# A third pair of k-tiles by Strassen's scheme in the second halves of the down projection

## The chip, the cores and the metric

The kernel runs on one core of a Trainium2 chip. The metric is the time of one execution on the device in microseconds (us); lower is better. A core has a matrix engine (TensorE, PE in the profile, with its weight loads as PEld), a vector engine (VectorE, DVE), a scalar engine (ScalarE, ACT), GpSimd (POOL) and SyncE (SP), which here only issues DMAs. TensorE accumulates into eight banks of PSUM of 128 x 512 fp32 numbers each; everything else lives in SBUF, with 128 partitions.

## The reference

One layer of a decoder block over 256 tokens with a model width of 2048, all in float32. A mixer of three branches (a conformer convolution, a short convolution, cross-attention into 256 memory tokens), gated and summed, goes through an output projection, and then comes an MLP. The change is in the MLP:

```
h = rms_norm(x, g_mlp_pre)                         # 256 x 2048
f = square(relu(h @ w_up)) @ w_down                # w_up 2048 x 8192, w_down 8192 x 2048
x = x + rms_norm(f, g_mlp_post)
```

## The kernel before

**Precision.** Every float32 factor is split into a high part and the remainder, both in a reduced fp32 type (`F32R`). A product of an activation tile and a weight tile is three matmuls: high by high, high by remainder, remainder by high. This text calls such three matmuls of 512 columns *a product*.

**Weights.** The list `units` is written out by `plan` and `plan_rows` ahead of the program, in the order in which TensorE will want the weights. `in_unit(u)` (L197) hands a unit to the matmuls and calls `fetch(u + LOOK)`, with `LOOK = 4`. Fetching a unit is: a 512 KB load issued by SP into one of six `raw` buffers, a cast on ScalarE to `wh` (L146), and a subtraction on VectorE to `wl` (L147). There are five buffers each of `wh` and `wl`.

**The MLP** runs in four blocks (`blk`, L930) of 2048 of the 8192 inner channels. In each, four groups of the up projection (`channels_first`, 64 matmuls of 512 columns and 64 of 256) fill four banks each. Their results are scaled, put through relu and square and split into `ft` (L940 to L948) while the next group runs. Then the down projection multiplies the block's 2048 channels, sixteen k-tiles of 128, into sums over the blocks in `acc2` (256 x 2048). It does so for the first 1024 columns (`n = 0`, the first halves) and then for the second 1024 (`n = 1`, the second halves), each with one call of `block` (L286, called at L963). In block 3 the second halves are done otherwise, by `tokens_first` for columns 1024 to 1535 and 1536 to 2047, which also ends the kernel.

**A call of `block`** covers 256 tokens (two tiles `t`) by 1024 columns (two halves `q` of 512). A k-tile done plainly, a *row*, is four products, one to each of the four accumulators C11, C12, C21, C22. A *pair* of k-tiles would be eight products; by Strassen's scheme (Winograd's form) it is seven. Its weights come in four units:

- `first` and `second` load the two rows of the pair. Only half of `first` is split. GpSimd then issues an accumulating DMA for each (L149, L151), SBUF to SBUF, that adds one half of a raw row to another; the second one writes into the buffer of the first.
- `outer` (L136 to L139) makes two sums of raw halves with two additions on VectorE, which need the first transfer, and splits them.
- `inner` splits what the two transfers left in the buffer of `first`.

The raw buffers of `first` and `second` are held that long. The activation side of these units are four sums of quarter tiles per pair, made by `down_sums` (L921) while the second up group's results are drained. Products that don't go to a C go to four more banks, P1, P6, P7 and Q5, so a block with pairs uses all eight. At the last of those products `gather` (block 0) or `gather_add` (the others) adds them into `acc2` on VectorE, and behind the block `after_down` (L907) adds the C banks.

**The order of a block's units** is made by `plan_rows` (L101): `lead` plain rows, then the four units of each pair, staggered, with the other rows between them, and one row at the end. With two pairs and `lead=4`, as in all down blocks before, a block has 62 products. The gate blocks of the mixer (`gates`, L665) use the same `block` and `fetch_row`; several of them have three pairs, with `lead=2`.

**Order on the engines.** Tile buffers come from pools (`t8`, 13 buffers of 8 KB per partition; `t1k`, six of 256 columns; small rings beside them). The instructions of each engine are ordered at build time by a planner with its own costs and by priorities: fetching goes ahead (`high_priority`), work in `soon()` further ahead.

Of the kernel before, what the change touches and what calls it, by code (L numbers as in the profile page):

```python
# [9 lines left out]
F32R = mybir.dt.float32r  # L10
# [5 lines left out]
P = 128  # L16
D = 2048
T = 256
KD = D // P
# [7 lines left out]
NC5 = 512  # L27
# [15 lines left out]
X_PAIRS = ((0, 8), (1, 9), (2, 10))  # L43
GATES = ((0, 3), (2, 3), (0, 3))
O_PAIRS = ((0, 4), (1, 5), (2, 6))
D_PAIRS = ((0, 4), (1, 5))
TQ = ((0, 0), (1, 0), (0, 1), (1, 1))
LOOK = 4
PRIO = 400
# [4 lines left out]
def tile_hybrid_block(ctx, tc, x, head, xT, mem, memT, vecs, w_in, w_a_out, w_b_out, w_kv, w_x_out, w_o,  # L54
# [19 lines left out]
    def t8(shape, dt=F32):  # L74
        return big.tile(shape, dt, tag="t8", name=name("t8"))

    def t1k(cols=T, bufs=6):
        return sm.tile([P, cols], F32, tag=f"t{cols}", name=name("s"), bufs=bufs)
# [22 lines left out]
    def plan_rows(w, row0, col0, nk, pairs=(), lead=2, hold=0):  # L101

        taken = [k for p in pairs for k in p]
        rows = [("row", k, None) for k in range(nk) if k not in taken]
        parts = [(4 * j + at, what, k, j) for j, (k0, k1) in enumerate(pairs)
                 for what, k, at in (("first", k0, 0), ("second", k1, 1), ("outer", k0, 4.5), ("inner", k0, 6.5))]
        parts = [p[1:] for p in sorted(parts)]
        order, among = rows[:lead], rows[lead:-1]  # L110
        for n, p in enumerate(parts):
            while n >= hold and among and (len(among) - 0.5) * (len(parts) - hold) >= (len(rows) - 1 - lead) * (len(parts) - n):
                order.append(among.pop(0))
            order.append(p)
        got = []
        for what, k, j in order + among + rows[-1:]:
            units.append((w, row0 + k * P, col0, (what, j), None))
            got.append((what, k, j, len(units) - 1))
        return got, pairs
# [166 lines left out]
    def block(rows, act, forms=None, gathered=None):  # L286

        todo = []
        rows, pairs = rows

        def tile_of(k, t):
            return lambda: [act(k)[:, i, t * P:(t + 1) * P] for i in range(2)]

        def form(j, i):
            return lambda: [f[:, j, i, :] for f in forms]

        for what, k, j, u in rows:  # L300
            if what == "row":
                todo += [(u, f"C{t + 1}{2 - q}", tile_of(k, t), q) for t, q in TQ]
            elif what == "first":
                todo.append((u, "P1", tile_of(k, 0), 1))
            elif what == "second":
                todo += [(u, "C11", tile_of(k, 0), 1), (u, "C12", form(j, 3), 0)]
            elif what == "outer":
                todo += [(u, "P6", form(j, 1), 0), (u, "C21", tile_of(pairs[j][1], 1), 1)]
            else:
                todo += [(u, "Q5", form(j, 0), 1), (u, "P7", form(j, 2), 0)]  # L310

        todo[:8] = sorted(todo[:8], key=lambda x: x[1])
        last = {x[1]: i for i, x in enumerate(todo)}
        end = max((i for c, i in last.items() if c[0] != "C"), default=None)
        acc = {}
        for i, (u, c, a, q) in enumerate(todo):
            wh, wl = in_unit(u)[q]
            ah, al = a()
            first = c not in acc
            if first:  # L320
                acc[c] = bank()
            mm(acc[c], ah, wh, first, False)
            mm(acc[c], ah, wl, False, False)
            mm(acc[c], al, wh, False, i == last[c])
            if i == end:
                with soon():
                    gathered(acc)
            if i % 8 == 7:
                between()
        return acc  # L330
# [31 lines left out]
    def split(src, dst_h, dst_l):  # L362
        nc.scalar.copy(dst_h, src)  # L363
        nc.vector.tensor_tensor(dst_l, src, dst_h.bitcast(F32), ALU.subtract)  # L364

    def pair(tiles):
        return lambda k: tiles[k // 4][:, k % 4]


    g_gate, g_y, g_up, g_dn = {}, {}, {}, {}  # L370
# [27 lines left out]
    for blk in range(4):  # L398
        for g in range(4):
            g_up[blk, g] = plan(w_up, 0, blk * D + g * NC5, gain=V_MLP)  # L400
        for n in range(2):
            if blk < 3 or n == 0:
                g_dn[blk, n] = plan_rows(w_down, blk * D, n * 2 * NC5, KD, D_PAIRS, lead=4)
    for n in (2, 3):
        g_dn[3, n] = plan(w_down, 3 * D, n * NC5)

# [57 lines left out]
    def over_partitions(r, dst):  # L464

        b = bank()
        for t in range(2):
            dg = t1k(P, bufs=2)
            nc.vector.tensor_scalar(dg, ident, r[:, t:t + 1], None, ALU.mult)
            mm(b[:, t * P:(t + 1) * P], ones, dg, t == 0, t == 1)  # L470
        nc.vector.tensor_copy(dst, b[:, :T])
# [232 lines left out]
    for i in range(2):  # L704
        cx = t8([P, 4, KB - 1 + T])
        nc.gpsimd.memset(cx[:, :, 0:KB - 1], 0.0)
        for c, b in enumerate(channels_first(g_sc[i], xg)):
            s = t1k()
# [212 lines left out]
    def down_sums(fd, j, qa, qb):  # L921

        s = t512().rearrange("p (i t) -> p i t", i=4)
        nc.vector.tensor_tensor(s[:, 0, :], qa[:, P:], qb[:, P:], ALU.subtract)
        nc.vector.tensor_tensor(s[:, 1, :], s[:, 0, :], qa[:, :P], ALU.subtract)
        nc.vector.tensor_tensor(s[:, 2, :], qa[:, :P], qa[:, P:], ALU.subtract)
        nc.vector.tensor_tensor(s[:, 3, :], qb[:, :P], s[:, 1, :], ALU.add)
        split(s, fd[:, 0, j], fd[:, 1, j])

    for blk in range(4):  # L930
        f, kept = [], []
        fd = t8([P, 2, len(D_PAIRS), 4, P], F32R)
        for g in range(4):
            first = blk == 0 and g == 0
            if first:
                steps += [stats_2, lambda: over_partitions(r2, r2_bc), keep_x2, load_gq]
            banks = channels_first(g_up[blk, g], pair(h2),
                                   late=turns if first else None)
            ft = t8([P, 4, 2, T], F32R)
            for c, b in enumerate(banks):  # L940
                s = t1k()
                halves(b, s)
                nc.vector.scalar_tensor_tensor(s, s, 0.0, r2_bc, ALU.max, ALU.mult)
                paired = c < len(D_PAIRS)
                q = (sm.tile([P, T], F32, tag="kept", name=name("q"), bufs=len(D_PAIRS)) if g == 0 and paired else t1k())
                nc.vector.tensor_tensor(q, s, s, ALU.mult)  # L946
                split(q, ft[:, c, 0, :], ft[:, c, 1, :])
                if g == 0 and paired:  # L948
                    kept.append(q)
                elif g == 1 and paired:  # L950
                    down_sums(fd, c, kept[c], q)
            f.append(ft)
        if blk == 3:
            res = [t8([P, D]) for _ in range(2)]
            for t in range(2):
                x2[t] = t8([P, D])
                nc.sync.dma_start(x2[t], x2_kept[t])
        forms = [fd[:, i] for i in range(2)]
        for n in range(2 if blk < 3 else 1):
            def part(t, q):  # L960
                return acc2[t][:, (2 * n + q) * NC5:(2 * n + q + 1) * NC5]

            acc = block(g_dn[blk, n], pair(f), forms,  # L963
                        lambda acc: gather(acc, part) if blk == 0 else gather_add(acc, part))
            for t, q in TQ:
                after_down(blk, 2 * n + q, t, acc[f"C{t + 1}{2 - q}"])
        for n in (2, 3) if blk == 3 else ():
            if n == 3:
                def none(acc):
                    pass  # L970

                def d_0(acc):
                    after_down(3, 3, 0, acc[0])
                    rf = row_rsqrt(ssf[0])
                    for n in range(3):
                        finish(0, rf, n * NC5, (n + 1) * NC5)
                    late_rf.append(rf)

                def d_1a(acc):
                    after_down(3, 3, 1, acc[1], 0, T)  # L980

                def d_1(acc):
                    after_down(3, 3, 1, acc[2], T, NC5)
                    rf = row_rsqrt(ssf[1])
                    with tc.issue_after(mean[0]):
                        finish(0, late_rf[0], 3 * NC5, D)
                    for c0, c1 in ((0, 256), (256, 768), (768, 1408), (1408, D)):
                        finish(1, rf, c0, c1)

                tokens_first(g_dn[blk, n], pair(f), late=[none, d_0, none, d_1a, d_1], fine=True)  # L990
            else:
                for t, b in enumerate(tokens_first(g_dn[blk, n], pair(f))):
                    after_down(blk, n, t, b)
# [37 lines left out]
```

## Time and profile before

| | |
|---|---|
| time, median of 3 runs | 1575.07 us (1574.99 to 1575.26) |
| the profiled execution's own time | 1574.08 us |
| its span, first to last instruction | 1572.2 us |
[...]
| PE busy | 1551.4 us, 99% |
| DVE busy | 1245.8 us, 79% |
| ACT busy | 831.5 us, 53% |
| DMA, mean | 206 GB/s |

The span is that of one execution under the profiler; the time of the runs is a little longer than the span, as the profiled execution's own time shows. Busy shares are means over stages with different limits, so a stage is read by itself. In the rows below a line such as `L147` is the line of the kernel that issued the instruction, `out<-in` names the tiles by the program's names, and `<-` behind an idle time names what ended it. For a matmul `bank<-wh,t` is a product whose weights stream (`block`, the down projection and the gates) and `bank<-t,wh` one whose activations stream (the up projection).

### The profile page before, as it was taken

The numbers are of one execution on the slowest core, as the hardware profiler recorded it, in microseconds if no ns is written. First come the engines' busy times: TensorE is split into PE (matmuls) and PEld (weight loads), VectorE is DVE, ScalarE is ACT, GpSimd is POOL, SyncE is SP. The second block draws the span as 40 slices with busy tenths as digits, with TensorE's granted clock in tenths as the row PEclk, the third lists the DMA queues.
The fourth block names the chain that finished last, engine by engine and source line by source line (L and its number), as shares of the span: only waits on it lengthen the run. The fifth ranks groups of instructions, "written<-read, shape, count | busy, mean of one in ns | idle before, by whom it ended". The sixth has DMA issues, their size and how long they took to land.

```text
span 1572.2 us, 21520 instructions
## 1 busy us (share of the span) xinstructions
PE 1551.4 (99%) x7866; PEld 1324.9 (84%) x7866; DVE 1245.8 (79%) x1883; ACT 831.5 (53%) x1170; POOL 55.6 (4%) x75
## 2 busy tenths in 40 slices
PE   8999999999999999999999999999999999999997
PEld 7888888888888888888788988888888888888886
DVE  7888787798898988778776787778778687777785
ACT  7654454554443545455555665456545555456552
POOL 0000000000000010000100000000000000000000
PEclk9999999999999999999999999999999999999999
DMA  9765555587666768558776665776577666776682
GB/s 321 221 206 190 190 163 172 159 234 223 189 189 174 229 187 286 181 174 237 226 259 196 221 191 175 228 240 191 167 234 232 202 190 199 208 236 189 207 259 81
DMA packets 132521, 324.54 MB, mean 206 GB/s; under 512 B 10432, under 2 KB 14784, under 8 KB 131392
## 3 DMA queue, kind: packets, MB, share of 16 engines
q1 hardware_dynamic: 124352, 308.50, 61.7%
q0 software_dynamic: 8064, 14.68, 5.4%
q8 instruction: 61, 1.00, 0.3%
q14 instruction: 44, 0.36, 0.1%
HBM read 304.26 MB, written 4.19 MB: 196 GB/s over the span
## 4 chain that ended last, share of the span: by engine, by line
PE 91%; DMA 3%; DVE 3%; issue 2%; ACT 0%; POOL 0%; SPq 0%; POOLq 0%; DVEq 0%; ACTq 0%
PE bank L84 90%; DMA raw<-raw 2%; DVE wl L147 1%; DMA raw<-in_w_o 1%; DMA t<-in_xT 0%; DMA raw<-in_w_down 0%; DVE t L833 0%; DVE t L364 0%; DVE raw L139 0%; DVE t L672 0%; PE bank L841 0%; ACT wh L146 0%; DVE t L918 0%; DVE wl L169 0%; DVE t L687 0%
## 5 line engine op out<-in xcount | busy, mean ns | idle before, releaser
L84 PE MATMUL bank<-wh,t 128*128 128x512 f32 (+1 forms) x2536 | 778.2, 387 | 0.0
L84 PEld LDWEIGHTS bank<-wh,t 128*128 128x128 f32 x2536 | 474.0, 188 | 96.6 <-DVE t L364 0.5
L146 ACT CAST wh<-raw 128x1024 fp32r<-128x1024 f32 (+1 forms) x328 | 330.2, 1017 | 330.7 <-PE bank L84 246.0
L84 PE MATMUL bank<-wl,t 128*128 128x512 f32 (+1 forms) x1268 | 490.4, 387 | 0.5 <-DVE wl L147 0.5
L84 PE MATMUL bank<-t,wh 128*128 128x512 f32 (+1 forms) x1936 | 464.5, 391 | 6.0 <-ACT wh L163 4.6
L147 DVE TENSOR_TENSOR wl<-raw,wh 128x1024 fp32r<-128x1024 f32 (+1 forms) x328 | 379.6, 1176 | 95.8 <-ACT wh L146 93.7
L84 PEld LDWEIGHTS bank<-t,wh 128*128 128x128 f32 x1936 | 354.9, 189 | 73.5 <-ACT wh L163 4.6
L84 PEld LDWEIGHTS bank<-wl,t 128*128 128x128 f32 x1268 | 238.2, 188 | 48.8 <-DVE wl L147 1.2
L84 PEld LDWEIGHTS bank<-t,wl 128*128 128x128 f32 x1936 | 248.7, 191 | 10.6 <-DVE wl L164 1.1
L163 ACT CAST wh<-raw 128x1024 fp32r<-128x1024 f32 (+1 forms) x161 | 168.1, 1046 | 165.7 <-PE bank L84 152.6
L164 DVE TENSOR_TENSOR wl<-raw,wh 128x1024 fp32r<-128x1024 f32 (+1 forms) x161 | 195.5, 1217 | 73.7 <-ACT wh L163 73.2
L84 PE MATMUL bank<-t,wl 128*128 128x256 f32 (+1 forms) x1936 | 252.0, 283 | 0.9 <-DVE wl L164 0.9
L169 DVE SCALAR_TENSOR_TENSOR wl<-raw,vec,wh 128x512 fp32r<-128x512 f32 x256 | 180.4, 747 | 46.2 <-ACT wh L168 45.7
L168 ACT ACTIVATE wh<-raw,vec 128x512 fp32r<-128x512 f32 x256 | 171.5, 717 | 76.1 <-PE bank L84 57.0
L596 DVE SCALAR_TENSOR_TENSOR t<-a_pad,vec,t 128x256 f32<-128x256 f32 x240 | 103.9, 482 | 0.0
L359 ACT COPY s<-bank 128x256 f32<-128x256 f32 x128 | 45.6, 368 | 54.6 <-PE bank L84 53.2
L360 DVE TENSOR_TENSOR s<-bank,s 128x256 f32<-128x256 f32 x128 | 51.7, 420 | 19.3 <-ACT s L359 19.3
L149 POOL DMA_DIRECT2D raw<-raw x28 | 24.4, 872 | 1025.3 <-DVE wl L147 1014.5
L363 ACT CAST t<-s 128x256 fp32r<-128x256 f32 x88 | 34.2, 401 | 37.7 <-DVE s L946 29.4
L138 DVE TENSOR_TENSOR raw<-raw,raw 128x512 f32<-128x512 f32 x28 | 19.3, 689 | 28.3 <-DMA raw<-raw 27.1
L364 DVE TENSOR_TENSOR t<-s,t 128x256 fp32r<-128x256 f32 x88 | 36.3, 421 | 5.0 <-ACT t L363 3.8
L151 POOL DMA_DIRECT2D raw<-raw x28 | 24.2, 863 | 127.1 <-DMA raw<-raw 108.8
(144 smaller groups left out, 530.6 us busy)
## 6 DMA issues: line engine op xcount, KB each, us to landing
raw<-in_w_in SPq DMA_DIRECT2D x191, 512.0 KB, 4.3
raw<-in_w_up SPq DMA_DIRECT2D x128, 512.0 KB, 4.0
raw<-in_w_down SPq DMA_DIRECT2D x128, 512.0 KB, 4.8
raw<-in_w_kv SPq DMA_DIRECT2D x32, 512.0 KB, 3.9
raw<-in_w_o SPq DMA_DIRECT2D x32, 512.0 KB, 5.3
raw<-raw POOLq DMA_DIRECT2D x56, 256.0 KB, 3.7
raw<-in_w_x_out SPq DMA_DIRECT2D x16, 512.0 KB, 4.6
raw<-in_w_b_out SPq DMA_DIRECT2D x16, 512.0 KB, 5.3
```

The costliest lines, as they stand in the source:

```text
L84: nc.tensor.matmul(o, a, b, start=start, stop=stop)
L146: nc.scalar.copy(h[:, part], raw[:, part])
L147: pace[0] = nc.vector.tensor_tensor(l[:, part], raw[:, part], h[:, part].bitcast(F32), ALU.subtract).ins
L163: nc.scalar.copy(h, raw)
L164: pace[0] = nc.vector.tensor_tensor(l, raw, h.bitcast(F32), ALU.subtract).ins
L168: nc.scalar.mul(h[:, j, :], raw[:, j, :], g)
L169: pace[0] = nc.vector.scalar_tensor_tensor(l[:, j, :], raw[:, j, :], g, h[:, j, :].bitcast(F32), ALU.mult, ALU.subtract).ins
L359: nc.scalar.copy(t, b[:, T:])
L360: nc.vector.tensor_tensor(dst, b[:, :T], t, ALU.add)
L363: nc.scalar.copy(dst_h, src)
L364: nc.vector.tensor_tensor(dst_l, src, dst_h.bitcast(F32), ALU.subtract)
L596: nc.vector.scalar_tensor_tensor(conv[:, c, :], src, w, conv[:, c, :], ALU.mult, ALU.add)
```

## The change

The second halves of the down projection in blocks 0 to 2 take a third pair of k-tiles, (2, 6), by Strassen's scheme, and have two plain rows ahead of the pairs in place of four. The first halves keep two pairs and four rows. The sums on the activation side are made for three pairs in every block, and are kept in two tiles (high and remainder) in place of one. The scratch of 128 columns in `over_partitions` is taken from the ring of 256 columns. The ring `kept`, sized by the number of pairs, has three buffers in place of two.

```
-D_PAIRS = ((0, 4), (1, 5))
+D_PAIRS = ((0, 4), (1, 5), (2, 6))
+DOWN = (2, 3)
...
-                g_dn[blk, n] = plan_rows(w_down, blk * D, n * 2 * NC5, KD, D_PAIRS, lead=4)
+                g_dn[blk, n] = plan_rows(w_down, blk * D, n * 2 * NC5, KD, D_PAIRS[:DOWN[n]], lead=4 - 2 * n)
...
-            dg = t1k(P, bufs=2)
+            dg = t1k()[:, :P]
...
-        split(s, fd[:, 0, j], fd[:, 1, j])
+        split(s, fd[0][:, j], fd[1][:, j])
...
-        fd = t8([P, 2, len(D_PAIRS), 4, P], F32R)
+        fd = [t8([P, len(D_PAIRS), 4, P], F32R) for _ in range(2)]
...
-        forms = [fd[:, i] for i in range(2)]
...
-            acc = block(g_dn[blk, n], pair(f), forms,
+            acc = block(g_dn[blk, n], pair(f), fd,
```

The units of a second-half block, with the product at which each starts (r: row, f, s, o, i: first, second, outer, inner unit of a pair):

```
before  r2 0, r3 4, r6 8, r7 12, f0 16, r8 17, s0 21, r9 23, f1 27, r10 28, o0 32, r11 34,
        s1 38, i0 40, r12 42, o1 46, r13 48, i1 52, r14 54, r15 58, end 62
after   r3 0, r7 4, f0 8, r8 9, s0 13, f1 15, r9 16, o0 20, s1 22, r10 24, i0 28, r11 30,
        f2 34, o1 35, r12 37, s2 41, i1 43, r13 45, o2 49, i2 51, r14 53, r15 57, end 61
```

## Rows read from the trace of the kernel before

**Rows 1.** The page, part 1: busy us of each engine, share of the span, instructions.
```profile
PE 1551.4 (99%) x7866; PEld 1324.9 (84%) x7866; DVE 1245.8 (79%) x1883; ACT 831.5 (53%) x1170; POOL 55.6 (4%) x75
```
**Rows 2.** Waits of PE over the whole span: us in total, times, longest.
```profile
PE bank L84 <- ACT wh L163: 4.6, 1, 4.6
...
PE bank L84 <- DVE wl L147: 0.5, 1, 0.5
```
**Rows 3.** Timeline of PE (start, us, what) where block 0 starts its down projection.
```profile
955.68 0.39 PE L84 MATMUL bank<-wh,t 128*128 128x512 f32 x1
```
**Rows 4.** Timeline of PE where block 0 of the MLP gives over to block 1.
```profile
1040.01 1.98 PE L84 MATMUL bank<-t,wh 128*128 128x512 f32 x8
```
**Rows 5.** Busy us by stage of the MLP; last: clock, DMA share, GB/s.
```profile
997.90:1040.00 42.10, 42.10 (x187) 34.86 (x186) 30.11 (x36) 21.65 (x25) 3.44 (x4) 1.00 0.74 223
...
1062.30:1084.60 22.30, 22.30 (x130) 19.70 (x129) 17.04 (x34) 13.02 (x24) 0.00 (x0) 1.00 0.63 189
1084.60:1106.90 22.30, 22.30 (x130) 19.70 (x129) 19.49 (x42) 14.07 (x26) 0.00 (x0) 1.00 0.65 190
1106.90:1129.10 22.20, 22.20 (x130) 19.61 (x129) 16.22 (x29) 11.87 (x20) 0.00 (x0) 1.00 0.61 189
...
1171.30:1213.40 42.10, 42.10 (x188) 34.85 (x187) 32.78 (x40) 21.64 (x25) 3.44 (x4) 1.00 0.73 218
...
1475.90:1518.10 42.20, 41.69 (x184) 34.22 (x183) 32.64 (x45) 22.62 (x28) 3.44 (x4) 1.00 0.82 251
```
**Rows 6.** DVE groups by shape, MLP blocks: busy us, mean ns, idle before.
```profile
L147 DVE TENSOR_TENSOR wl<-raw,wh 128x1024 fp32r<-128x1024 f32 x112 | 135.5, 1222 | 47.8 <-ACT wh L146 46.4
...
L138 DVE TENSOR_TENSOR raw<-raw,raw 128x512 f32<-128x512 f32 x12 | 8.3, 689 | 9.1 <-DMA raw<-raw 9.1
L147 DVE TENSOR_TENSOR wl<-raw,wh 128x512 fp32r<-128x512 f32 x12 | 8.3, 688 | 2.7 <-ACT wh L146 2.6
...
L364 DVE TENSOR_TENSOR t<-u,t 128x512 fp32r<-128x512 f32 x8 | 5.5, 685 | 0.0
...
L924 DVE TENSOR_TENSOR u<-q,s 128x128 f32<-128x128 f32 x8 | 2.3, 286 | 0.0
```
**Rows 7.** ACT groups by shape, MLP blocks.
```profile
L146 ACT CAST wh<-raw 128x1024 fp32r<-128x1024 f32 x112 | 117.5, 1055 | 109.5 <-PE bank L84 104.9 <-DVE wl L147 2.0 <-DVE raw L138 1.6
...
L146 ACT CAST wh<-raw 128x512 fp32r<-128x512 f32 x12 | 7.5, 623 | 16.0 <-PE bank L84 16.0
```
**Rows 8.** DMA issues while the second halves of block 1 run: KB, median us to landing.
```profile
q0 software_dynamic: 576, 1.05, 14.0%
...
raw<-raw POOLq DMA_DIRECT2D x4, 256.0 KB, 3.6
```
**Rows 9.** Busy us by stage: two gate blocks with three pairs each.
```profile
311.10:352.60 41.50, 41.50 (x185) 34.37 (x184) 38.24 (x55) 22.53 (x23) 4.47 (x6) 1.00 0.81 225
...
571.80:613.30 41.50, 41.50 (x185) 34.35 (x183) 38.59 (x45) 22.41 (x23) 4.35 (x5) 1.00 0.84 250
```
**Rows 10.** Timeline of PE where the first of branch 1's gate blocks starts.
```profile
507.90 0.39 PE L84 MATMUL bank<-wh,t 128*128 128x512 f32 x1
```
**Rows 11.** Timeline of DVE in a gate block with three pairs: the third outer unit.
```profile
598.08 0.69 DVE L138 TENSOR_TENSOR raw<-raw,raw 128x512 f32<-128x512 f32 x1 [0.95 <-DMA raw<-raw]
...
599.41 5.76 DVE L147 TENSOR_TENSOR wl<-raw,wh 128x1024 fp32r<-128x1024 f32 x5
```
**Rows 12.** Timeline of POOL in the same gate block.
```profile
589.12 0.87 POOL L149 DMA_DIRECT2D raw<-raw  x1 [4.77 <-DMA raw<-in_w_in]
598.27 0.87 POOL L151 DMA_DIRECT2D raw<-raw  x1 [8.28 <-DMA raw<-raw]
```
**Rows 13.** Chain that ended last, in order of time, in the last block.
```profile
1478.01 9.14 DMA raw<-raw
```
**Rows 14.** Timeline of SP in the MLP: DMA issues.
```profile
1475.05 0.90 SPq L957 DMA_DIRECT2D t<-x_kept  x2
```
**Rows 15.** Timeline of DVE where block 1 passes from first to second halves.
```profile
1173.33 2.48 DVE L910 TENSOR_TENSOR t<-bank,t 128x512 f32<-128x512 f32 x4
```

## The prediction

> **What bounds the kernel now.** I read the page first. TensorE is busy for 99% of the span, VectorE for 79%, ScalarE for 53% [rows 1]. Then the waits of PE, because a busy engine can still be the wrong one: there are seven kinds of wait in the whole span, from 4.6 us (once, at the start of the kernel) down to 0.5 us [rows 2], and that last one, half a microsecond on VectorE's `wl`, is the only one in the whole MLP. The stages say the same: in both shown stages of second halves PE is busy for 42.10 of 42.10 us, at a granted clock of 1.00, while VectorE has 30.1 and 32.8 us of work and ScalarE 21.6 [rows 5]. So in the stage that the diff changes, the end is set by how many matmuls are issued and at what pitch; everything else is cover.
>
> The pitch: in block 0, the two down blocks run from 955.68 [rows 3] to 1040.01 [rows 4], 84.33 us. By the code each is 12 plain rows of 12 matmuls and two pairs of 21, so 186, together 372. 84.33 / 372 = 226.7 ns for one 512-column matmul, or 0.680 us for a product of three. (The mean duration that the profile gives one matmul is longer; consecutive ones overlap, so the pitch and not the duration prices a removed one.)
>
> **The change, part by part.**
>
> *Matmuls.* Two plain rows are eight products; a Strassen pair is seven. A third pair in the second halves of blocks 0 to 2 takes one product from each: 3 x 3 = 9 matmuls, 9 x 0.2267 = 2.04 us, all of it on PE, which waits for nothing there [rows 5]. Block 3 has no second-half block of this form and loses nothing. Bounds: 2.04 us if PE stays full, 0 if what follows is late by as much. I take 2.04.
>
> [...]
>
> *Splits and sums behind the products, per changed block.* Two plain rows cost VectorE 2 x 1.22 = 2.44 us. A pair costs a half split 0.69, two full splits 2.44, the outer's two adds 1.38 and its split 1.22, 5.73 us together [rows 6]. That is 3.29 us more: 32.8 becomes 36.1 us in a stage of 41.5 (42.1 less one product), 87%. ScalarE gets 0.62 + 3 x 1.06 - 2 x 1.06 = 1.68 us more [rows 7], 23.3 of 41.5. Neither becomes the bound. The nearest rows are two gate blocks of the same kernel with the same order: three pairs behind two rows, 61 products. There VectorE had 38.2 and 38.6 us of work in 41.5, and PE was busy for 41.50 of 41.50 in both [rows 9]. I take 0 on the path. Upper bound: the one down block in which PE did lose time, that of block 3, lost 0.51 us (42.20 less 41.69) [rows 5]; three times that is 1.5 us.
>
> *DMAs.* The loads stay at sixteen rows per block. Each changed block issues two more accumulating DMAs from POOL, 256 KB each, and POOL issues one in 0.87 us [rows 12]. Four such transfers were 14.0% of the sixteen DMA engines' time in a second-half stage and landed after a median 3.6 us [rows 8]; six make about 21%, so the DMA share goes from 0.73 to about 0.80. The gate blocks, with six, ran at 0.81 and 0.84 [rows 9]. 0 on the path, the same upper bound as above. POOL's queue does hold something behind them: the second transfer of a pair waits on POOL for the first one's landing, 8.28 us in one gate block [rows 12], and with it the inner unit.
>
> *The shorter lead.* With two rows ahead of the pairs and not four, the first pair's P1 starts after 8 products of the block instead of 16, 5.4 us in. It needs a ninth bank, one that the first halves' results leave. Those were added away by 1173.33 + 2.48 = 1175.8 [rows 15], against a P1 at 1171.3 + 5.4 = 1176.7, and P1 needs the first bank of the four, free some 1.8 us earlier. The first outer of the second halves is needed at product 20, 13.6 us in; the first unit's split, on which its transfer waits, takes the weight buffer that the fifth unit before it leaves (there are five), here the last inner unit of the first halves, which ends 8 products before the block starts. 0.
>
> *The third set of sums on the activations.* `down_sums` runs once more in every block, block 3 too, where only two sets are used: VectorE 4 x 0.286 + 0.685 = 1.83 us [rows 6], ScalarE a cast of some 0.62 [rows 7], by the same shape. It falls where VectorE is fullest in the up projection, the stage behind the second group: 19.49 of 22.30 us become 21.3, with 1.0 us of cover left; the next has 16.22 of 22.20 [rows 5]. What is late there is the draining of banks whose next user is a group later, 22.3 us, and the sums themselves, not needed before the down projection. 0; if all of it reached PE, 4 x 1.83 = 7.3 us.
>
> *Buffers.* The sums in two tiles instead of one take a twelfth of thirteen large buffers during a block (four of h2, two of acc2, four of f, now two of sums). In blocks 1 to 3 the new block's buffers are first written a group after the old ones are read last, so nothing waits. In block 3 two result tiles and the reload of x2 come on top, and now one more of them waits for a buffer of h2. The reload is issued at 1475.05 [rows 14], when only the last of the four h2 tiles (products 12 to 15 of the up group ending at 1475.9) is in use; the third has been free for some 5 us. 0, between -0.5 us (if it moves away from the transfers of that block's first pair, and the 0.51 us of idle go) and +1.5 us (if it falls on more of them). The 128-column scratch now comes from the 256-column ring of six: `over_partitions` writes it twice in each of its four calls, behind evacuations that have ended or are ending. 0, upper bound one wait of the middling kind seen, about 1 us.
>
> *Sum.* 1572.20 - 2.04 = 1570.2 us of span; 1574.08 - 2.04 = 1572.0 us for the profiled execution. The median of the runs is 1575.07, 1.0 us above the profiled one, so the forecast of the median is **1573.0 us**, 0.13% faster. What a measurement of this kernel tells from no change is about 0.2%, 3.15 us: I forecast a real gain that stays inside that bound.
>
> **The rivals.**
>
> *A late accumulation makes PE wait in the second halves (slower).* Place: third pair, outer (product 49) and inner (product 51). The outer's adds on VectorE wait for the first transfer, the inner's for the second, and behind an add in VectorE's queue stand the splits of later rows. For: VectorE did wait for such transfers, 9.1 us in twelve outers [rows 6], and in block 3 one took 9.14 us [rows 13]. Against, in numbers: the second gate block of branch 1 started at 507.90 + (62 + 32) x 0.680 = 571.8 [rows 10]. Its third first-transfer was issued at 589.12 [rows 12] and freed the adds at 598.08 [rows 11], 9.0 us later. Adds to 599.5, cast 1.06 and split 1.22 end at 601.8; PE needs it at 571.8 + 49 x 0.680 = 605.1. The five splits in a row end at 605.2 [rows 11], PE needs the inner at 606.5: 1.3 us to spare even behind a 9.0 us landing, where the stage that changes had 3.6. The point from which it decides: a wait of 0.68 us a block cancels the gain, a landing of 9.0 + 1.3 + 0.7 = 11 us; slower by 0.2% needs 2.04 + 3.15 = 5.2 us, 1.7 us a block, a landing of 12 us in all three. Then 1578.2. Chance 0.09.
>
> [...]
>
> *VectorE is the bound behind the second up group (slower).* If the 1.0 us of cover is not where the splits need it, PE waits for weights: with half of the 1.83 us exposed, 4 x 0.9 = 3.7 us, 1576.7; with all, 1580.3. Against: the splits are planned ahead of the draining, and gate blocks at 93% of VectorE left PE full [rows 9]. Chance 0.06.
>
> *The gain is hidden.* If another chain set the stage's end, nine matmuls less would give idle time and 1575.1. Against: no wait of PE in it. Chance 0.05.
>
> *Block 3 or the scratch buffers shift.* 1572.5 to 1575.1 by the bounds above. Chance 0.07.
>
> **How the numbers follow.** The forecast has 0.70, the four rivals 0.27; the 0.03 left are for queues that fall into a better order and close some of the waits outside the MLP. Range: 1572.2 to 1575.3 holds the forecast with 0.8 us below it, the hidden gain, the shift and the milder late accumulations, a little over 8 in 10. Slower by over 0.2% (above 1578.2) are about half of the first rival and half of the second, 0.08; faster by over 0.2% needs 3.15 us, 1.1 more than the matmuls hold, 0.03; the rest, 0.89, is inside.
>
> **What the profile after would show.** 9 matmuls fewer, 7857. The second-half stages of blocks 0 to 2 41.5 us long, PE busy throughout; all others as long as before. VectorE near 36 us there. Six POOL transfers in each. Wrong would be: PE waiting on `wl` or ScalarE's `wh` around products 49 to 51, in the stage behind the second up group, or at P1 on a bank; or stages of 42.1 us with idle time in them.

## The result and the profile after

The changed kernel takes **1587.28 us** (median of 6 runs, 1582.24 to 1592.33), the kernel before 1574.88 us beside it (median of 6). The ratio is 1.008, 95% interval 1.0067 to 1.0092: 12 us slower, where 2 us faster was forecast and 1575.3 was the upper end of the range. The runs spread over 10 us, where those of before spread over 1.4 us.

The page of the changed kernel has the matmuls that were forecast, 7857, nine fewer than in [rows 1]. Yet PE is busy 6.3 us longer, which is the second thing to explain beside the idle time:

```profile
PE 1557.7 (98%) x7857; PEld 1327.6 (83%) x7857; DVE 1257.7 (79%) x1915; ACT 837.7 (53%) x1180; POOL 60.8 (4%) x81
```

The waits of PE in the changed kernel, whole span (in total, times, longest). The 0.5 us on `wl` in [rows 2] have become 12.3 us in four waits; the wait at the start is as before:

```profile
PE bank L85 <- DVE wl L148: 12.3, 4, 4.7
PE bank L85 <- ACT wh L164: 4.8, 1, 4.8
```

The stages, PE busy first, then PEld, DVE, ACT, POOL, granted clock, DMA share, GB/s. The second, the fourth and the first row are the second halves of blocks 1, 2 and 0; the last row is block 3's first down stage, and the row between is four microseconds out of block 1's:

```profile
998.00:1043.60 45.60, 43.32 (x184) 35.43 (x183) 33.17 (x39) 23.62 (x27) 4.29 (x5) 0.96 0.75 217
1174.90:1223.70 48.80, 44.06 (x184) 35.98 (x183) 35.27 (x43) 23.51 (x27) 4.29 (x5) 0.93 0.73 210
1205.00:1209.00 4.00, 3.83 (x9) 3.09 (x10) 4.00 (x5) 0.14 (x1) 0.00 (x0) 0.50 0.73 194
1354.90:1401.60 46.70, 43.44 (x185) 35.44 (x184) 35.37 (x43) 23.39 (x27) 4.30 (x5) 0.96 0.75 219
1490.60:1536.00 45.40, 43.33 (x184) 35.36 (x183) 33.20 (x46) 22.71 (x28) 3.46 (x4) 0.96 0.80 242
```

The three stages were to be 41.5 us (61 products of 0.680). Taken from their first matmul to the first of the next stage they are 45.66, 48.81 and 46.63 us, 16.7 us over that in sum. PE's own idle time in them is 2.28, 4.74 and 3.26 us, 10.3 us; the other 6.4 us are matmuls at a lower clock. Behind the wait in block 1 the granted clock is 0.50 of full speed for the four microseconds shown, and its mean over the stage is 0.93. Everything from block 3's first down stage to the end is 3.5 us longer (99.9 us against 96.4), 1.55 of it idle time and the other 2.0 again slower matmuls. Together 16.7 - 2.0 + 3.5 = 18.2 us, where the span grew by 18.3 (1590.5 - 1572.2). The longer busy time is explained with it: 6.4 + 2.0 us of slower matmuls, less the 2.0 us of those that are gone, make the 6.3. The profiled execution was the slowest of the six; a second one, below, has the same four waits with 10.2 us.

Where the wait sits: PE's timeline in block 1, whose second halves start at 1174.9:

```profile
1199.82 0.61 PE L85 MATMUL bank<-wh,t 128*128 128x512 f32 x2
1205.17 0.80 PE L85 MATMUL bank<-wl,t 128*128 128x512 f32 x1 [4.74 <-DVE wl L148]
1205.76 1.06 PE L85 MATMUL bank<-wh,t 128*128 128x512 f32 x2
...
1207.04 1.06 PE L85 MATMUL bank<-wh,t 128*128 128x512 f32 x2
```

The first matmul of a product (with `wh`) has run at 1199.82, and the next, with `wl`, has to wait for VectorE. That is 25.2 us into the stage, product 37: plain row 12. Three matmuls take 1.28 us behind the wait (1205.76 to 1207.04), where they took 0.68. ScalarE had cast that row's `wh` long before:

```profile
1194.17 1.05 ACT L147 CAST wh<-raw 128x1024 fp32r<-128x1024 f32 x1 [1.66 <-PE bank L85]
```

And VectorE, the releaser, was not busy. Its timeline:

```profile
1190.62 3.14 DVE L148 TENSOR_TENSOR wl<-raw,wh 128x1024 fp32r<-128x1024 f32 x3 [0.34 <-ACT wh L147]
1202.56 0.69 DVE L139 TENSOR_TENSOR raw<-raw,raw 128x512 f32<-128x512 f32 x1 [8.80 <-DMA raw<-raw]
1203.29 0.69 DVE L140 TENSOR_TENSOR raw<-raw,raw 128x512 f32<-128x512 f32 x1
1203.90 3.49 DVE L148 TENSOR_TENSOR wl<-raw,wh 128x1024 fp32r<-128x1024 f32 x3
```

VectorE sat idle for 8.80 us, until 1202.56, in front of L139, the first addition of the third outer unit, waiting for an accumulating transfer. Row 12's subtraction, 1.2 us of work whose inputs were there at 1195.2, came out of the queue only behind both additions. The build's instruction order shows why; VectorE's queue in block 1 (names with what they are):

```
L139 raw_10910<-raw_10826,raw_10872     outer 2, first addition: wanted for product 49
L140 raw_10910<-raw_10910,raw_10872     outer 2, second addition
L148 wl_10861<-raw_10858,wh_10860       row 12: wanted for product 37
L148 wl_10875<-raw_10872,wh_10874       second 2: wanted for product 41
L148 wl_10892<-raw_10715,wh_10891       inner 1: wanted for product 43
```

Why the planner puts the additions first is not shown; they need no `wh` buffer, and by its own costs their transfer may have landed by then. In the trace VectorE kept to this order: 8.80 us of idle time in front of the first addition, with row 12's subtraction ready behind it.

### The profile page after: what moved, and what is told of

The parts are those of the page before. It is cut to its first block, busy times and chain, and to the rows that moved or that the text cites. A ratio compares the mean times of both kernels' runs of the same rounds, so it can differ in the third digit from the quotient of the medians.

```text
span 1590.5 us, 21571 instructions
## 1 busy us (share of the span) xinstructions
PE 1557.7 (98%) x7857; PEld 1327.6 (83%) x7857; DVE 1257.7 (79%) x1915; ACT 837.7 (53%) x1180; POOL 60.8 (4%) x81
## 4 chain that ended last, share of the span: by engine, by line
PE 84%; DMA 7%; DVE 5%; issue 4%; ACT 1%; SPq 0%; POOL 0%; DVEq 0%; POOLq 0%; ACTq 0%
PE bank L85 83%; DMA raw<-raw 4%; DVE wl L148 2%; DMA raw<-in_w_down 1%; DMA raw<-in_w_in 1%; DMA raw<-in_w_o 1%; ACT wh L147 1%; DVE raw L139 0%; DVE t L834 0%; DVE raw L140 0%; DVE t L365 0%; DVE t L673 0%; DVE t L919 0%; DVE wl L170 0%; PE bank L842 0%
## 5 line engine op out<-in xcount | busy, mean ns | idle before, releaser
L85 PE MATMUL bank<-wl,t 128*128 128x512 f32 (+1 forms) x1265 | 492.6, 389 | 12.4 <-DVE wl L148 12.3
L85 PEld LDWEIGHTS bank<-t,wl 128*128 128x128 f32 x1936 | 249.2, 192 | 10.3 <-DVE wl L165 0.7
L170 DVE SCALAR_TENSOR_TENSOR wl<-raw,vec,wh 128x512 fp32r<-128x512 f32 x256 | 180.2, 748 | 41.5 <-ACT wh L169 41.4
L150 POOL DMA_DIRECT2D raw<-raw x31 | 27.0, 871 | 1014.7 <-DVE wl L148 973.2
L139 DVE TENSOR_TENSOR raw<-raw,raw 128x512 f32<-128x512 f32 x31 | 21.4, 689 | 46.6 <-DMA raw<-raw 45.1
L152 POOL DMA_DIRECT2D raw<-raw x31 | 26.7, 862 | 145.6 <-DMA raw<-raw 126.6
```

Source lines behind the costliest of these rows:

```text
L85: nc.tensor.matmul(o, a, b, start=start, stop=stop)
L170: pace[0] = nc.vector.scalar_tensor_tensor(l[:, j, :], raw[:, j, :], g, h[:, j, :].bitcast(F32), ALU.mult, ALU.subtract).ins
```

## The experiments

Theory A is this order. Against it stood B (the transfers are too late for their own products, whatever the order), C (the buffers or the third sums) and D (the shorter lead, or too much work on VectorE). The runs were made in three groups, each beside the kernel before on the same chip (medians 1574.57, 1574.32 and 1574.30 us).

**Additions of the third pair later.** The change is the place of two instructions in VectorE's queue: `issue_after(pace[0])` holds them behind the split of the unit before, here row 13. The build's order is the same for all other engines; on VectorE a few instructions at the end of each of these stages move by some places too.

```
+            with tc.issue_after(pace[0]) if j == 2 and w is w_down else ExitStack():
                 nc.vector.tensor_tensor(raw[:, 0], a[:, 1], b[:, 0], ALU.add)
                 nc.vector.tensor_tensor(raw[:, 1], raw[:, 0], b[:, 1], ALU.add)
```

> The changed kernel, with the two additions of the third pair's outer unit held in VectorE's queue until the split of the row before that unit has been issued (four splits later than now); nothing else differs. Theory A (queue order): in the changed kernel these additions wait for the first transfer of the third pair (7.6 to 9.8 us in the profile) and the split of row 12, wanted by PE at product 37, stands behind them. Then PE waits for nothing in the three second-half stages, each is about 41.5 us long, and the median is 1573 to 1576.5 us (the span before less 2 us, plus what block 3 loses by itself, 0 to 3.5 us). Theory B (the transfer itself is too late for its own product 49, or the second one for product 51): PE still waits 2 to 5 us per stage and the median stays above 1583 us.

Measured: 1574.92 us, ratio to before 1.0004 (0.9996 to 1.0013). The order alone gives twelve microseconds back. Block 2's second halves as a stage, PE's waits on `wl` over the span, and in the same stage POOL's two transfers of the third pair and VectorE behind them (line numbers one or two higher than before, by lines added):

```profile
1344.70:1386.20 41.50, 41.50 (x185) 34.38 (x184) 34.90 (x42) 23.28 (x27) 4.30 (x5) 1.00 0.84 238
```

```profile
PE bank L85 <- DVE wl L149: 3.4, 2, 2.6
```

```profile
1363.32 0.86 POOL L151 DMA_DIRECT2D raw<-raw  x1 [3.59 <-DVE wl L149]
1370.16 0.86 POOL L153 DMA_DIRECT2D raw<-raw  x1 [5.99 <-DMA raw<-raw]
```

```profile
1366.05 1.23 DVE L149 TENSOR_TENSOR wl<-raw,wh 128x1024 fp32r<-128x1024 f32 x1 [1.50 <-ACT wh L148]
1368.17 1.23 DVE L149 TENSOR_TENSOR wl<-raw,wh 128x1024 fp32r<-128x1024 f32 x1 [0.90 <-ACT wh L148]
...
1372.96 0.69 DVE L140 TENSOR_TENSOR raw<-raw,raw 128x512 f32<-128x512 f32 x1
```

The stage is the forecast 41.5 us with PE full. The first transfer was issued at 1363.32, and the second, which waits for its landing, left POOL at 1370.16, 6.8 us later; in the meantime VectorE made two splits, and when the addition came up at 1372.96 nothing was left to wait for. The 6.8 us are short of the 8.2 of the changed kernel's profile, but the landing is not what changed: the run with four holds, below, has 8.9, 8.2 and 8.9 us and no wait at row 12. So B falls as the cause of the long waits. Of the two waits that are left, 2.60 us stand in block 3, which the hold didn't touch. The other, 0.76 us in block 1, is B's own, on a small scale: it stands at product 51, the inner, whose cast on ScalarE had to wait for the second transfer:

```profile
1204.78 2.94 ACT L148 CAST wh<-raw 128x1024 fp32r<-128x1024 f32 x3 [3.04 <-DMA raw<-raw]
1207.14 0.50 PE L85 MATMUL bank<-wl,t 128*128 128x512 f32 x1 [0.76 <-DVE wl L149]
```

**Two pairs, everything else changed.**

```
-DOWN = (2, 3)
+DOWN = (2, 2)
...
-    D_PAIRS[:DOWN[n]], lead=4 - 2 * n)
+    D_PAIRS[:DOWN[n]], lead=4)
```

> The changed kernel with two pairs and four rows ahead in the second halves as before: what is left of the change is the third set of sums on the activations (made and not used), the sums in two tiles, the three kept buffers and the scratch from the common ring. Theory A: these cost nothing, 1575 us within 1 us, PE waits about 0.5 us in block 3. Theory C (the buffers or the third sums shift something, block 3's additional 3.5 us above all): 1577 to 1579 us, with a PE wait of some 2 us in block 3's down stage.

Measured: 1574.83 us, ratio 0.9999 (0.9990 to 1.0008), one wait of 0.91 us in block 3. C falls: third sums, buffers and scratch cost nothing that shows (the interval leaves some 1.5 us either way), as the prediction had them.

**The first transfer of the third pair as an addition on VectorE.**

```
+            if j == 2 and w is w_down:
+                nc.vector.tensor_tensor(raw[:, 1], raw[:, 1], raw[:, 0], ALU.add)
+            else:
                 nc.gpsimd.dma_start(raw[:, 1], raw[:, 0], accum_op=ALU.add)
```

> The changed kernel, with the first of the third pair's two accumulating transfers replaced by one VectorE addition right behind that unit's split (0.69 us more of VectorE per stage); the place of the outer's additions in the queue stays. Theory A and B both say the wait on the transfer is the cause: with nothing to wait for, PE is full, 1573 to 1576.5 us. Theory D (VectorE has too much work in the stage, or the shorter lead is at fault): waits of PE stay or grow, above 1583 us.

Measured: 1572.19 us, ratio 0.9986 (0.9977 to 0.9994), by the medians 2.4 us faster than before. VectorE has more work and the lead is still two rows, so D falls. Its queue in block 1, with the new addition at L151:

```profile
1187.95 0.69 DVE L151 TENSOR_TENSOR raw<-raw 128x512 f32<-128x512 f32 x1
...
1194.48 0.69 DVE L139 TENSOR_TENSOR raw<-raw,raw 128x512 f32<-128x512 f32 x1 [4.70 <-DMA raw<-in_w_down]
```

The outer's additions still stand where they stood, and still wait, but for the load of the second row (4.70 us); PE loses 0.73 us there, and 1.8 us in the whole MLP.

**Four rows ahead of the three pairs.**

```
-    D_PAIRS[:DOWN[n]], lead=4 - 2 * n)
+    D_PAIRS[:DOWN[n]], lead=4)
```

> The changed kernel with four rows ahead of the three pairs instead of two. Theory D (the shorter lead is at fault): the waits go, 1573 to 1576.5 us. Theory A: the third outer's additions again stand in VectorE's queue ahead of the second unit's split of that pair, which PE wants at product 41, 27.9 us into the stage; the first unit can be split from 20.4 us on, its transfer lands at 29.5 to 32, and PE waits some 3 to 5 us in each of the three stages: 1583 to 1595 us.

Measured: 1591.2 us, ratio 1.0103 (1.0087 to 1.0118). The longer lead does not help, as the order says: the third outer's additions now stand ahead of the second unit's split (product 41). PE's waits, and VectorE in block 2:

```profile
PE bank L85 <- DVE wl L148: 13.3, 4, 5.6
```

```profile
1385.43 0.69 DVE L139 TENSOR_TENSOR raw<-raw,raw 128x512 f32<-128x512 f32 x1 [7.93 <-DMA raw<-raw]
```

**All additions later, in the changed kernel and in the kernel before.** In both, the same `with` line without its condition.

> The changed kernel with the additions of every outer unit of the kernel (gates, output projection, down projection) held in VectorE's queue behind the split of the unit before. Theory A (queue order) says that block 3's wait has the same cause as those of the second halves: the second pair's additions wait for a transfer and the next row's split stands behind them. So this wait goes too, no PE wait above 0.5 us is left in the MLP, and the median is 1571 to 1573.5 us, 1.5 to 3 us under the kernel before. Rival: block 3's wait comes from the reload of x2 delaying the loads and transfers themselves; then a wait of 1 to 3 us stays in block 3 and the median is like that of the single hold, 1574 to 1575.5 us.

> The kernel before with the additions of every outer unit held in the same way, two pairs everywhere. Tells what the order alone is worth without the third pair. Theory A: only block 3's wait (0.5 us in its profile, perhaps more in other executions) can go: 1573 to 1574.6 us. If holding the additions costs something in the gates or the output projection, it is slower than before.

Measured: 1578.06 us, ratio 1.0024 (1.0015 to 1.0034), and 1578.06 us, 1.0026 (1.0016 to 1.0037). Both times were forecast wrong. Block 3's wait did go in both, as theory A said and its rival denied. But more is lost ahead of the MLP, where the additions of the gates and the output projection are held: the last transposes there start at 868.90 and 868.86 us, where they started at 863.16 before. In the first of the two, PE waits:

```profile
PE bank L793 <- DVE t L366: 3.1, 1, 3.1
PE bank L85 <- DVE wl L149: 2.1, 2, 1.4
```

The 3.1 us at L793 is a transpose in the output projection (1.0 us there before), and the longer of the two waits in the next row stands in a gate block; both are ahead of the MLP. In the second kernel the wait at the transpose is 4.0 us. The stretch with branch 1's gate blocks is 2.6 us longer in both (140.9 us against 138.3). That is not all of the 5.7 us, and in the first kernel 3.3 us are there already 63 us into the execution, long before the first outer unit; the rest was not followed. In the MLP of the first kernel 0.72 and 0.76 us, on ScalarE and on VectorE, are left in block 2, at the third inner, where the cast waits for the second transfer: more than the 0.5 us that theory A allowed. The second kernel has no wait in the MLP.

**Three pairs in the first halves too, all additions later.**

```
-DOWN = (2, 3)
+DOWN = (3, 3)
...
-    D_PAIRS[:DOWN[n]], lead=4 - 2 * n)
+    D_PAIRS[:DOWN[n]], lead=2)
```

> The changed kernel with every outer's additions held as in the run above, and three pairs behind two rows in the first halves too (four blocks more, 12 matmuls less, 2.7 us). Theory A: the saved matmuls come through where PE has no waits: 2.7 us under the run with all additions held, 1568.5 to 1571 us. Rival (the transfers themselves are too late when all down blocks have three): waits of 1 us and more in several stages and no gain, 1573 us or more.

Measured: 1579.22 us, ratio 1.0040 (1.0028 to 1.0053), a miss: not faster than the run with two pairs there. PE waits seven times in five down stages, 0.17 to 0.76 us each, 4.1 us together, against 2.7 us of matmuls saved. The rival of this run is the nearer one, though no wait reaches the 1 us that it named: with three pairs everywhere weights come late even with the additions held. In both stages of block 1 the cast of the inner waits for the pair's second transfer (2.24 and 2.09 us on ScalarE).

**VectorE sums at the four places that stalled.** The condition is now `w is w_down and (j == 2 or r0 >= 3 * D and j == 1)`: the third pairs, and block 3's second pair. No addition is held.

> The changed kernel with the places of all additions as the planner has them, and the first accumulating transfer replaced by one VectorE addition for the third pair of the second halves and for the second pair of block 3. Theory A: no addition waits for a late transfer in the places that stalled, so no PE wait above 0.8 us in the MLP; 1570.5 to 1572.5 us. Rival (block 3's wait is the reload's): like the run with the third pair's sum on VectorE, 1572 us or more, with a wait in block 3.

Measured: 1572.29 us, ratio 0.9988 (0.9979 to 0.9997), one wait of 1.04 us, in block 2, over the 0.8 that theory A allowed; none in block 3. The wait is at row 12 again: the additions still stand ahead of its split, and now wait for the load of the second row (4.81 us). The time fits both of its theories; by the wait in block 3 it is theory A.

**The hold at these four places alone, and with the VectorE sums.** The second kernel adds the diff of the run before.

```
+            with tc.issue_after(pace[0]) if w is w_down and (j == 2 or r0 >= 3 * D and j == 1) else ExitStack():
                 nc.vector.tensor_tensor(raw[:, 0], a[:, 1], b[:, 0], ALU.add)
                 nc.vector.tensor_tensor(raw[:, 1], raw[:, 0], b[:, 1], ALU.add)
```

> The changed kernel with the additions held behind the split of the unit before at four places only: the third pair of the second halves of blocks 0 to 2, and the second pair of block 3. Theory A: these are the places where a split that PE wants sooner stood behind additions that waited for a transfer; the order elsewhere, gates and output projection, is as the planner has it. So the waits there go and none come in their stead: 1571 to 1573 us, PE waits in the MLP of 1.5 us at most together. If block 3's wait stays, 1574 to 1575 us as with the single hold.

> The run with VectorE sums in place of four first transfers, and with the additions of the same four pairs held as well. Theory A: what little PE still waits for there (1.0 us in block 2) goes; 1570.5 to 1572.3 us, the fastest of all or equal to the run without the hold.

Measured: 1572.35 us, ratio 0.9993 (0.9984 to 1.0001), and **1571.66 us, ratio 0.9981 (0.9972 to 0.9990)**, the lowest median of all; the first of the two intervals still holds no change. The hold alone leaves PE one wait in the list for the MLP, in front of a bank of the next up projection, and about 0.3 us at the third inner of block 2, too short for the list. Its third pairs' first transfers are as late as ever, in block 2 8.9 us (1359.57 to 1368.46, where the second leaves POOL), which without the hold would have been some 3.6 us of waiting by the sum below:

```profile
PE bank L85 <- DVE u L355: 0.3, 1, 0.3
```

```profile
1359.57 0.86 POOL L151 DMA_DIRECT2D raw<-raw  x1 [4.50 <-DVE wl L149]
1368.46 0.86 POOL L153 DMA_DIRECT2D raw<-raw  x1 [8.03 <-DMA raw<-raw]
```

With both, no wait is left in the MLP; 50 us that take in block 0's second halves:

```profile
990.00:1040.00 50.00, 50.00 (x222) 41.40 (x221) 40.88 (x48) 26.62 (x31) 4.31 (x5) 1.00 0.78 233
```

**The changed kernel again.**

> The changed kernel once more, for a second profile. Theory A: a PE wait on VectorE's split in each of the three second-half stages at product 37, 1 to 5 us each, its size set by when the third pair's first transfer lands in that execution (7 to 10 us after its issue), and a lower granted clock behind it; 1582 to 1592 us.

Measured: 1588.03 us, ratio 1.0087 (1.0075 to 1.0100). The profile has the same four places, 2.55, 3.04 and 1.95 us in blocks 0 to 2 and 2.67 us in block 3:

```profile
PE bank L85 <- DVE wl L148: 10.2, 4, 3.0
```

The third pairs' first transfers took 8.2, 8.2 and 6.6 us in it; in the first profile 7.5, 9.7 and 8.2, where the waits go up and down with them. In the second the two longest are alike, and the one issued later in its stage (17.2 us in block 0, 17.8 in block 1) has the longer wait.

## Why the prediction was wrong

*Matmuls: right.* Nine fewer, and where PE is kept full they are worth the 2.04 us. The stages show it best: block 0's two down blocks took 84.33 us before, and take 83.64 us with hold and sums together, blocks 1 and 2 likewise (84.32 before, 83.64 each).

```profile
956.70 0.39 PE L85 MATMUL bank<-wh,t 128*128 128x512 f32 x1
...
1040.34 1.98 PE L85 MATMUL bank<-t,wh 128*128 128x512 f32 x8
```

The medians go the same way, 1.95 us with the hold at four places, 2.4 us with the VectorE sum, 2.6 us with both, but with runs that spread by 3 to 5 us they can't tell 1 us from 3, and with the four places part of the gain is block 3's.

*VectorE's and ScalarE's work, buffers, bank of P1, third sums: right.* 33 to 35 us of VectorE's work in the stages against 36.1, no wait on a bank at the shorter lead, and 1574.83 against 1574.57 us with only these parts of the change.

*The step that failed is the price of the late accumulation, the first rival.* The mechanism was named: additions that wait for a transfer, with the splits of later rows behind them in VectorE's queue. But it was then priced by the products of the outer and inner themselves, 49 and 51, and not by those of the splits behind. With the row's own product, 37, the landing from which PE waits shrinks from 10.3 us (9.0 + 1.3) to about 5: the third pair's first transfer is issued some 17.7 us into the stage (1015.66 with a start at 998.0), the additions and the split take 2.4 us, and the split is wanted at 25.4 us. 25.4 - 17.7 - 2.4 leaves 5.3 us for the landing, and all six seen, 6.6 to 9.7 us, are longer. What is over agrees with the waits: in the first profile landings of 7.5, 9.7 and 8.2 us give 2.2, 4.4 and 2.9 us, measured 2.28, 4.74 and 3.26. The chance of 0.09 was on the right event at the wrong point. At the point that the prediction did price, the inner at product 51, the runs with the hold waited in single stages, 0.3 to 1.5 us.

*The rows that stood for this stage didn't have its queue.* The gate block of branch 1 [rows 11, 12] had a landing of 9.0 us and a full PE, and was read as proof of a margin. Its VectorE queue has row 12's and the second unit's splits ahead of the third outer's additions: another order from the same list of units, why is not shown. The two other gate blocks with three pairs are nearer to the changed stages, with the first of the two additions ahead of row 12's split. There VectorE waits too; from the kernel before:

```profile
333.87 0.69 DVE L138 TENSOR_TENSOR raw<-raw,raw 128x512 f32<-128x512 f32 x1 [2.51 <-DMA raw<-raw]
334.48 2.35 DVE L147 TENSOR_TENSOR wl<-raw,wh 128x1024 fp32r<-128x1024 f32 x2
```

That block started at 311.1 (counted back by products from its branch's end at 374.3), so row 12's split was wanted at 336.4, and the first of these two splits ends near 335.7: under one microsecond to spare, on a landing of 5.3 us (issued at 328.55), and with only one addition ahead. This is what the second halves should have been compared with. Landings of the third pairs' first transfers, the chain of the changed kernel (start, us; two gate blocks, then the second halves of blocks 0 to 2):

```profile
329.49 6.19 DMA raw<-raw
...
722.25 5.34 DMA raw<-raw
...
1015.66 7.49 DMA raw<-raw
...
1192.75 9.73 DMA raw<-raw
...
1372.81 8.24 DMA raw<-raw
```

*A landing of 3.6 us was taken from two-pair stages [rows 8].* It is a median over the first and second transfers of both pairs; the third pair's first transfers take 1.5 to 2.5 times that in the gates (5.3 to 9.0 us) and 1.8 to 2.7 times here. In the changed stages the first transfers are later from pair to pair: from their issue to that of the second transfer it was 3.6, 5.4 and 10.0 us in block 1, and 3.6 to 3.9, 5.1 to 5.4 and 7.8 to 10.0 us over the three blocks. Why is open. In block 1 of the changed kernel the sixteen DMA engines had little to do in the second half of VectorE's wait (rows of two stretches of it, DMA share in the column before the last):

```profile
1192.70:1197.70 5.00, 5.00 (x24) 4.14 (x23) 1.06 (x1) 1.05 (x1) 0.86 (x1) 1.00 0.86 208
1197.70:1202.50 4.80, 2.73 (x13) 1.92 (x11) 0.00 (x0) 3.42 (x4) 0.00 (x0) 1.00 0.33 70
```

Their mean load at that moment, 0.33, doesn't explain it; that of a single engine is not in these rows. No run took this apart.

*Not priced at all: the clock.* In the first profile each of the four waits, 2.07 to 4.74 us, was followed by a stretch at a lower clock (granted clock 0.50 to 0.64 over the next four microseconds, 0.50 in block 1), with 1.9, 2.6 and 1.9 us lost in the three stages, 6.4 us beside 10.3. But not every such wait did this: behind 1.95 us in block 2 of the second profile, and behind the 3.15 us at a transpose with all additions held, the granted clock was 1.00, while behind the 4.03 us at the same transpose in the kernel before with the additions held it was 0.50. Behind the 0.52 us wait of before, in block 3, it stayed at 1.00. Why some waits did this and others did not is not shown. Four microseconds behind each of the first three (granted clock in the third column from the end):

```profile
1379.50:1383.50 4.00, 4.00 (x18) 3.27 (x19) 4.00 (x5) 1.06 (x1) 0.00 (x0) 1.00 0.80 215
...
790.30:794.30 4.00, 3.97 (x20) 3.37 (x21) 3.43 (x5) 3.43 (x5) 0.86 (x1) 1.00 0.78 247
...
788.00:792.00 4.00, 3.96 (x12) 3.31 (x13) 3.35 (x5) 2.58 (x3) 0.86 (x1) 0.50 0.85 257
```

*Block 3:* put at -0.5 to +1.5 us for the buffers, it lost 3.5 us in the profile. The buffers weren't it: with all of them and two pairs the wait is 0.91 us, and VectorE's queue there is the same in the kernel before. It is the same mechanism one row earlier: the second outer's first addition stands ahead of the split of row 11, wanted at product 34. In the changed kernel:

```profile
1514.32 0.69 DVE L139 TENSOR_TENSOR raw<-raw,raw 128x512 f32<-128x512 f32 x1 [6.29 <-DMA raw<-raw]
1514.93 1.22 DVE L148 TENSOR_TENSOR wl<-raw,wh 128x1024 fp32r<-128x1024 f32 x1
...
1516.20 0.50 PE L85 MATMUL bank<-wl,t 128*128 128x512 f32 x1 [2.07 <-DVE wl L148]
```

With two pairs there, the wait went whenever these additions were held or their transfer replaced. Why the kernels with third transfers from POOL waited longer there (2.07 and 2.67 us, and 1.82 to 2.60 in two experiments, against 0.52 to 0.91 in three kernels without) is open.

## What to carry to other kernels

When an instruction that waits for a DMA enters the queue of an engine that keeps to its order, as VectorE did here (8.80 us idle in front of an addition, 1.2 us of ready work behind it), the deadline that counts is that of the most urgent instruction queued behind it, so read the queue of the stage itself, not that of a stage with the same list of work. A comparison stage proves a margin only if the engine's order is the same there too. Where a planner orders by its own DMA costs, pin such an instruction behind the urgent ones or feed it from the engine itself, and only there: pinned everywhere, the same hold cost 3.7 us.

## What was not expected of the hardware

An accumulating transfer of 256 KB within SBUF landed after 3.6 us in some places and after 6.6 to 9.7 us in others of the same kernel, with the DMA engines at a share of 0.33 towards the end of one. And a stall of 2.3 us cost 4.2 us, since 1.9 us of slower matmuls came behind it (granted clock 0.57 in the four microseconds that followed in block 0). So this stall cost nearly twice its length, where one of 1.95 us in the second profile had none of this behind it (granted clock 1.00).
